# A tiled transpose: hand-made synchronisation, 256-byte aligned tiles, and stores that read 16 KB at a time

## The chip, the cores and the metric

The kernel runs on one core of a Trainium2 chip. The metric is the time of one execution on the device in microseconds (us), taken over several runs. A second number, the span, is the length of the profiled execution; in one and the same run the time is about 1.8 us longer than the span.

A ratio between two kernels is the mean time of one kernel's fast runs over the mean of the other's fast runs of the same rounds, so it is not quite the ratio of the medians that stand beside it.

## The reference

```python
def setup_inputs():
    return {"x": np.random.randn(8192, 8192).astype(np.float32)}

def reference(x):
    return np.transpose(x)
```

There are 268 MB to read and 268 MB to write, 537 MB through the DMA engines, and no arithmetic.

## The kernel before

The matrix is cut into 32 blocks of 1024 x 2048. A block is loaded by two DMAs whose contiguous runs are 8 KB (2048 floats of a row of `x`). TensorE transposes it in 128 x 128 pieces, eight to a PSUM tile of 128 x 1024. ScalarE (ACT) and VectorE (DVE) in turn copy these tiles to SBUF. Four copies fill an output tile, in which every partition holds four rows of 4 KB; one DMA stores it. A scheduler places the tiles and makes the semaphores.

```python
    R, C, G, LS = 8, 16, 4, 2          # (four lines in the kernel)
    I, J = R * P, C * P                # 1024 x 2048
    const_pool = ctx.enter_context(tc.tile_pool(name="const", bufs=1))
    in_pool = ctx.enter_context(tc.tile_pool(name="in_pool", bufs=2))
    out_pool = ctx.enter_context(tc.tile_pool(name="out_pool", bufs=4))
    psum_pool = ctx.enter_context(tc.tile_pool(name="psum", bufs=4, space=bass.MemoryType.PSUM))
    ident = const_pool.tile([P, P], dt)
    # ... cut: for each block
            in_tile = in_pool.tile([P, R, J], dt)
            for s in range(LS):
                src = x[i0 + s * rs * P:i0 + (s + 1) * rs * P, j0:j0 + J]
                src = src.rearrange("(a p) j -> p a j", p=P)
                nc.sync.dma_start(out=in_tile[:, s * rs:(s + 1) * rs, :], in_=src)
            for g in range(C // G):
                out_tile = out_pool.tile([P, G, I], dt)
                # ... cut: four times eight transposes into ps, one copy of ps to out_tile
                dst = out[j0 + g * G * P:j0 + (g + 1) * G * P, i0:i0 + I]
                dst = dst.rearrange("(b q) i -> q b i", q=P)
                nc.scalar.dma_start(out=dst, in_=out_tile)
```

Two facts about addresses matter. The first SBUF bytes of the kernel's own are four small constants (128 bytes) and the identity (512 bytes), so every input and output tile begins 128 bytes past a multiple of 256 (in the built program the first input tile lies at byte 17024 of a partition, 66 x 256 + 128). And although the four rows of an output tile lie side by side in SBUF, the stores are recorded as 65536 packets of 4096 bytes, one for each row.

## Time and profile before

| | before |
|---|---|
| time, median of the first 3 runs | 1279.18 us |
| span | 1276.3 us |
| DMA rate over the span | 421 GB/s |
| PE, DVE, ACT busy | 55%, 25%, 20% |

From the page of the kernel before: the mean busy share of the 16 DMA engines in tenths and the rate, each in 40 equal slices of the span; then the two queues with packets, MB and the time of their packets as a share of 16 engines (q1 is the loads, q10 the stores); then, for each kind of DMA, how many, the size and the median time from issue to landing.

```profile
DMA  9999999999999999999999999999999999999999
GB/s 392 425 423 424 425 423 425 423 422 424 423 422 423 424 424 423 424 422 423 424 424 422 422 422 424 424 423 423 423 423 424 422 422 422 424 424 423 422 422 375
...
q10 hardware_dynamic: 67584, 268.44, 51.4%
q1 hardware_dynamic: 33792, 268.44, 49.8%
...
in_tile<-in_x_dram SPq DMA_DIRECT2D x64, 4096.0 KB, 27.9
out_dram<-out_tile ACTq DMA_DIRECT2D x128, 2048.0 KB, 28.9
```

The engines that move data are busy 90% or more in every slice, and the rate is flat. This is a DMA-bound kernel: only a higher steady rate, or less time at the two ends, can shorten it.

The waits of the kernel before (who waited for what: us in total, times, longest):

```profile
ACT out_tile L69 <- DMA out_dram<-out_tile: 832.2, 97, 14.2
PEld ps L63 <- DVE out_tile L71: 605.9, 247, 9.7
DVE out_tile L71 <- DMA out_dram<-out_tile: 593.7, 81, 11.7
```

The copies wait for stores to give output tiles back. So stores lag and loads are ahead: a backlog of stores is queued. By the packet records stores move at least 119 GB/s in every 2 us from 32 to 1274 us.

The end of the kernel before, in five stretches of its span (stretch; length; busy time and number of instructions for PE, PEld, DVE, ACT, POOL; granted clock; DMA share; GB/s):

```profile
1210.00:1230.00 20.00, 9.03 (x40) 8.12 (x40) 3.67 (x3) 3.85 (x4) 0.00 (x0) 0.63 1.02 426
1230.00:1240.00 10.00, 6.78 (x39) 6.02 (x38) 3.67 (x3) 1.93 (x2) 0.00 (x0) 0.71 1.02 419
1240.00:1250.00 10.00, 7.33 (x62) 6.38 (x59) 3.99 (x4) 4.05 (x4) 0.00 (x0) 1.00 1.02 421
1250.00:1260.00 10.00, 6.77 (x56) 6.06 (x56) 4.58 (x4) 3.44 (x4) 0.00 (x0) 1.00 1.03 419
1260.00:1280.00 20.00, 1.09 (x8) 0.86 (x8) 1.23 (x2) 0.61 (x1) 0.00 (x0) 0.62 0.66 271
```

The packet records put the end of the last load's data at 1232.8 us. For 27 us after it, to 1260 us, the DMA engines still run at about 420 GB/s: the backlog covers the time in which the last block is transposed.

### The profile page before, as it was taken

Reading aid. Unit: us, or ns where it says so; the run is one execution under the profiler, and the core shown is the slowest. Engines: PE = TensorE matmul, PEld = TensorE weight load, DVE = VectorE, ACT = ScalarE, POOL = GpSimd, SP = SyncE. Lnnn points to the kernel's source line nnn. Section 1 sums busy time; section 2 is a strip of 40 time slices with the busy share of each in tenths; the row PEclk is TensorE's granted clock in tenths of the full one; section 3 lists DMA queues with packets and bytes.
Section 4 is the critical chain, followed back from the end, with each engine's and each line's share of the span. In section 5 each row is a group of like instructions: output and inputs, shape, how many; then the busy total and the mean of one; then the engine's idle time right before and its main releaser. Section 6 shows DMA issues by size and latency. Waiting matters only on the chain.

```text
span 1276.3 us, 9511 instructions
## 1 busy us (share of the span) xinstructions
PE 700.7 (55%) x4096; PEld 629.0 (49%) x4096; DVE 313.5 (25%) x256; ACT 252.8 (20%) x257; POOL 0.7 (0%) x6
## 2 busy tenths in 40 slices
PE   3555555655565545655556555555555655556463
PEld 3454455544554544544445554454444544445453
DVE  1222223222232222322123221222222322122222
ACT  1221112121121211212112121221211212112121
POOL 0000000000000000000000000000000000000000
PEclk8777777767777677776677766878667777677867
DMA  9999999999999999999999999999999999999999
GB/s 392 425 423 424 425 423 425 423 422 424 423 422 423 424 424 423 424 422 423 424 424 422 422 422 424 424 423 423 423 423 424 422 422 422 424 424 423 422 422 375
DMA packets 101418, 537.49 MB, mean 421 GB/s; under 512 B 3072, under 2 KB 3072, under 8 KB 68608
## 3 DMA queue, kind: packets, MB, share of 16 engines
q10 hardware_dynamic: 67584, 268.44, 51.4%
q1 hardware_dynamic: 33792, 268.44, 49.8%
q8 instruction: 32, 0.52, 0.1%
q14 instruction: 10, 0.08, 0.0%
HBM read 268.44 MB, written 268.44 MB: 421 GB/s over the span
## 4 chain that ended last, share of the span: by engine, by line
DMA 89%; PE 6%; DVE 3%; issue 0%; ACT 0%; DVEq 0%; ACTq 0%; SPq 0%
DMA out_dram<-out_tile 87%; PE ps L63 6%; DVE out_tile L71 3%; DMA in_tile<-in_x_dram 2%; ACT out_tile L69 0%; DVEq L71 0%; ACTq L69 0%; SPq L55 0%
## 5 line engine op out<-in xcount | busy, mean ns | idle before, releaser
L63 PE MATMUL ps<-ident,in_tile 128*128 128x128 f32 x4096 | 700.7, 344 | 560.5 <-DVE out_tile L71 535.3
L63 PEld LDWEIGHTS ps<-ident,in_tile 128*128 128x128 f32 x4096 | 629.0, 181 | 631.9 <-DVE out_tile L71 605.9
L71 DVE COPY out_tile<-ps 128x1024 f32<-128x1024 f32 x256 | 313.5, 1225 | 948.9 <-DMA out_dram<-out_tile 593.7
L69 ACT COPY out_tile<-ps 128x1024 f32<-128x1024 f32 x256 | 251.5, 1014 | 1007.1 <-DMA out_dram<-out_tile 832.2
L69 ACT ACT_TABLE_LOAD x1 | 1.3, 1283 | 0.7 <-PEq L91 0.7
masks.py:199 POOL TENSOR_SCALAR_AFFINE_SELECT ident<-ident 128x128 f32<-128x128 f32 x1 | 0.3, 292 | 0.1
masks.py:197 POOL MEMSET ident<- 128x128 f32 x1 | 0.2, 204 | 0.3 <-POOLq L91 0.3
L91 POOL MEMSET const-bfloat16-1.0<- 128x1 bf16 x1 | 0.1, 101 | 0.0
L91 POOL MEMSET const-uint8-127<- 128x1 uint8 x1 | 0.1, 101 | 0.0
L91 POOL MEMSET const-float32-0.0<- 128x1 f32 x1 | 0.1, 98 | 0.2 <-issue 0.2
L91 POOL MEMSET const-float32-1.0<- 128x1 f32 x1 | 0.1, 98 | 0.0
## 6 DMA issues: line engine op xcount, KB each, us to landing
in_tile<-in_x_dram SPq DMA_DIRECT2D x64, 4096.0 KB, 27.9
out_dram<-out_tile ACTq DMA_DIRECT2D x128, 2048.0 KB, 28.9
```

The lines of the kernel that those rows point to most:

```text
L63: nc.tensor.transpose(ps[:, a * P:(a + 1) * P], in_tile[:, a, b * P:(b + 1) * P], ident,)
L69: nc.scalar.copy(out=out_tile[:, bb, :], in_=ps)
L71: nc.vector.tensor_copy(out=out_tile[:, bb, :], in_=ps)
L91: nc = _bacc.Bacc("TRN2", target_bir_lowering=False, num_devices=1)
```

## The change

The intent is to raise the DMA rate. The tiles are allocated by hand behind a pad of 128 bytes, so that they are 256-byte aligned (the first input tile now lies at byte 17152, 67 x 256). A store is given a source of one 16 KB run for each partition and a destination of four 4 KB rows. The last store stays as it was. Semaphores are written by hand. Tile sizes, numbers of buffers, loads and arithmetic are the same. The core of the diff, with cuts marked:

```diff
+def wide_dma(nc, eng, queue, out, in_):
+    return eng.add_instruction(
+        mybir.InstDMACopy(mode="Copy", name=nc.get_next_instruction_name(), engine=eng.engine,
+            ins=[physical(in_)], outs=[physical(out)], queue=queue))   # physical(): cut
...
-    ident = const_pool.tile([P, P], dt)
-    make_identity(nc, ident)
+    with tc.tile_critical():
+        nc.alloc_sbuf_tensor("pad", [P, 32], dt)
+        ident = nc.alloc_sbuf_tensor("ident", [P, P], dt).ap()
+        ins = [nc.alloc_sbuf_tensor(f"in_tile{k}", [P, R, J], dt).ap() for k in range(NIN)]
+        outs = [nc.alloc_sbuf_tensor(f"out_tile{k}", [P, G * I], dt).ap() for k in range(NOUT)]
+        pss = [nc.alloc_psum_tensor(f"ps{k}", [P, I], dt).ap() for k in range(NPS)]
...
+            if k >= NIN:
+                nc.sync.wait_ge(s_pe, (k - NIN + 1) * C)
...
+                    if n >= NPS:
+                        nc.tensor.wait_ge(s_cp[(n - NPS) % 2], (n - NPS) // 2 + 1)
...
+                    if bb < 2 and ouse > 0:
+                        eng.wait_ge(s_st[ob], 16 * ouse)
...
-                nc.scalar.dma_start(out=dst, in_=out_tile)
+                if ng < NG:
+                    st = wide_dma(nc, nc.scalar, "qActDynamicHW", dst, outs[ob])
+                else:
+                    st = nc.scalar.dma_start(out=dst, in_=outs[ob])
+                st.then_inc(s_st[ob], 16)
```

More of the change, by code (lines that the diff above doesn't have):

```diff
@@ L8, with physical @@
 from concourse._compat import with_exitstack
+def physical(ap):
+    t = ap.tensor
+    dims = [list(d) for d in ap.ap]
+    if len(dims) == 2:
+        dims.insert(1, [dims[1][1], 1])
+    return mybir.PhysicalAccessPattern(
+        ap=dims,
+        offset=ap.offset,
+        dtype=ap.dtype,
+        memref=t.name,
+        memsetref=t.name + "_set",
+    )
+def wide_dma(nc, eng, queue, out, in_):
+    return eng.add_instruction(
+        mybir.InstDMACopy(
+            mode="Copy",
+            name=nc.get_next_instruction_name(),
+            engine=eng.engine,
+            ins=[physical(in_)],
+            outs=[physical(out)],
+            queue=queue,
+        )
+    )
 @with_exitstack
@@ L30 @@
     LS = 2
-    const_pool = ctx.enter_context(tc.tile_pool(name="const", bufs=1))
-    in_pool = ctx.enter_context(tc.tile_pool(name="in_pool", bufs=2))
-    out_pool = ctx.enter_context(tc.tile_pool(name="out_pool", bufs=4))
-    psum_pool = ctx.enter_context(tc.tile_pool(name="psum", bufs=4, space=bass.MemoryType.PSUM))
-    ident = const_pool.tile([P, P], dt)
-    make_identity(nc, ident)
-    n_bi = N // I
-    n_bj = M // J
-    copy_idx = 0
-    for bj in range(n_bj):
-        j0 = bj * J
-        for bi in range(n_bi):
-            i0 = bi * I
-            in_tile = in_pool.tile([P, R, J], dt)
-            rs = R // LS
+    NIN = 2
@@ new lines @@
+    NOUT = 4
+    NPS = 4
+    with tc.tile_critical():
[4 more added lines that the diff above has]
+        pss = [nc.alloc_psum_tensor(f"ps{k}", [P, I], dt).ap() for k in range(NPS)]
+        s_id = nc.alloc_semaphore("s_id")
+        s_ld = [[nc.alloc_semaphore(f"s_ld{k}_{s}") for s in range(LS)] for k in range(NIN)]
+        s_st = [nc.alloc_semaphore(f"s_st{k}") for k in range(NOUT)]
+        s_pe = nc.alloc_semaphore("s_pe")
+        s_cp = [nc.alloc_semaphore("s_cpa"), nc.alloc_semaphore("s_cpv")]
+        nc.gpsimd.memset(ident, 0.0).then_inc(s_id, 1)
+        nc.gpsimd.wait_ge(s_id, 1)
+        nc.gpsimd.affine_select(
+            out=ident,
+            in_=ident,
+            compare_op=mybir.AluOpType.not_equal,
+            fill=1.0,
+            base=0,
+            pattern=[[-1, P]],
+            channel_multiplier=1,
+        ).then_inc(s_id, 1)
+        nc.tensor.wait_ge(s_id, 2)
+        blocks = [(bi, bj) for bj in range(M // J) for bi in range(N // I)]
+        rs = R // LS
+        n = 0
+        ng = 0
+        NG = len(blocks) * (C // G)
+        for k, (bi, bj) in enumerate(blocks):
+            slot, use = k % NIN, k // NIN
+            i0, j0 = bi * I, bj * J
+            in_tile = ins[slot]
+            if k >= NIN:
+                nc.sync.wait_ge(s_pe, (k - NIN + 1) * C)
@@ L52 @@
             for s in range(LS):
                 src = x[i0 + s * rs * P:i0 + (s + 1) * rs * P, j0:j0 + J]
-                src = src.rearrange("(a p) j -> p a j", p=P)
-                nc.sync.dma_start(out=in_tile[:, s * rs:(s + 1) * rs, :], in_=src)
+                nc.sync.dma_start(
+                    out=in_tile[:, s * rs:(s + 1) * rs, :],
+                    in_=src.rearrange("(a p) j -> p a j", p=P),
+                ).then_inc(s_ld[slot][s], 16)
             for g in range(C // G):
-                out_tile = out_pool.tile([P, G, I], dt)
+                ob, ouse = ng % NOUT, ng // NOUT
@@ L59 @@
+                ng += 1
                 for bb in range(G):
                     b = g * G + bb
-                    ps = psum_pool.tile([P, R * P], dt)
+                    ps = pss[n % NPS]
+                    e = n % 2
+                    eng = (nc.scalar, nc.vector)[e]
+                    if n >= NPS:
+                        nc.tensor.wait_ge(s_cp[(n - NPS) % 2], (n - NPS) // 2 + 1)
                     for a in range(R):
-                        nc.tensor.transpose(
+                        if b == 0 and a % rs == 0:
+                            nc.tensor.wait_ge(s_ld[slot][a // rs], 16 * (use + 1))
+                        ins_t = nc.tensor.transpose(
@@ L67 @@
                         )
-                    if copy_idx % 2 == 0:
-                        nc.scalar.copy(out=out_tile[:, bb, :], in_=ps)
-                    else:
-                        nc.vector.tensor_copy(out=out_tile[:, bb, :], in_=ps)
-                    copy_idx += 1
+                    ins_t.then_inc(s_pe, 1)
+                    eng.wait_ge(s_pe, n + 1)
+                    if bb < 2 and ouse > 0:
+                        eng.wait_ge(s_st[ob], 16 * ouse)
+                    o = outs[ob][:, bb * I:(bb + 1) * I]
+                    if e == 0:
+                        c = nc.scalar.copy(out=o, in_=ps)
+                    else:
+                        c = nc.vector.tensor_copy(out=o, in_=ps)
+                    c.then_inc(s_cp[e], 1)
+                    n += 1
                 dst = out[j0 + g * G * P:j0 + (g + 1) * G * P, i0:i0 + I]
+                nc.scalar.wait_ge(s_cp[0], n // 2)
+                nc.scalar.wait_ge(s_cp[1], n // 2)
                 dst = dst.rearrange("(b q) i -> q b i", q=P)
-                nc.scalar.dma_start(out=dst, in_=out_tile)
+                if ng < NG:
[3 more added lines that the diff above has]
+                st.then_inc(s_st[ob], 16)
+        for ob in range(NOUT):
+            nc.sync.wait_ge(s_st[ob], 16 * (ng // NOUT))
 _INS = ['x']
```

## The prediction

> What bounds it now. The slice table of the profile page has the DMA engines at 90% or more in all 40 slices and 422 to 425 GB/s in all but the first (392) and last (375). PE is busy 55%, DVE 25%, ACT 20%; the chain of waits that ended last is 87% stores. So the 16 DMA engines are the limit. The queue table gives loads 49.8% of their time for 32768 packets of 8 KB (310 ns each) and stores 51.4% for 65536 of 4 KB (160 ns). In the trace's packet records 8 KB loads start 306 ns apart and 4 KB stores 155.3 ns apart on an engine, with a small bubble every few packets.
>
> [...] bubbles cost about 3 ns per load and 1 per store.
>
> What the change does. (1) Tiles now start 128 bytes off a 256-byte boundary (512-byte identity behind 128 bytes of constants); the pad aligns them. [...] the runtime's own 8 KB packets take 309 ns beside the loads, as these do. So I am unsure that alignment helps. (2) A store reads 16 KB once and writes four rows: [...] (3) Hand-made semaphores make PE, ACT and DVE wait for exactly what they need; they matter only after the last load lands. Loads, tiles, buffers and arithmetic stay.
>
> Costs, estimated from those packets, per engine 2048 loads and 4096 store rows: 2048 x 309 + 4096 x 156 = 1272 us now. [...]
>
> What is given back. With both queues full, loads now move 283 GB/s and stores 140: the engine alternates packets, 8 KB against 4 KB. If it alternates 16 KB against 8 KB, stores win two thirds, the backlog of stores that covers the tail is gone, and after the last load the DMA waits for the first four tiles: 4 x 0.86 us of PE and a 1.23 us copy, 5 us.
>
> Sum: both gains and the tail loss 1257 us, without the loss 1252; stores alone 1267 and 1262; no gain, up to 1284. I say 1260 us, 1.5% faster; 8 in 10 within 1247 to 1277. Chances: faster by over 2% 0.30, within 2% 0.66, slower 0.04.
>
> What would show it. Steady slices at 428 to 432 GB/s. Store packets below 153 ns per 4 KB, about 610 ns if recorded as 16 KB. Loads at 305 ns if alignment matters, unchanged if not. More waits of PE for loads, fewer of ACT and DVE for stores; a last slice below 375 GB/s if the tail loses.
>
> What would make it wrong. A cost per written row instead of per read: no gain from wide reads. [...] Alignment worth more than I see. A tail loss that does not come, or is larger because PE's clock is throttled.

Two terms of the sum are cut from this text, together with the ceiling that they were worked out from, because no run here shows the figures that they rest on: what the wide reads and what the aligned loads were each to save. By the totals that are left, they came to 17 us (1284 to 1267) and 10 us (1267 to 1257). With both, and with the 5 us given back at the end, the sum came to 1257 us; the forecast was 1260. The signs of 428 to 432 GB/s and of 153, 610 and 305 ns follow from the cut terms too.

## The result

| | before | changed |
|---|---|---|
| median time (4 runs each) | 1279.2 us | 1276.62 us |
| ratio, with 95% interval | | 0.9976 (0.996 to 0.9993) |
| span | 1276.3 us | 1275.1 us |
| DMA rate over the span | 421 GB/s | 421 GB/s |

The kernel became 0.24% faster where 1.5% was forecast. The lines of the changed kernel's page and waits that answer to those above:

```profile
DMA  9999999999999999999999999999999999999996
GB/s 393 417 430 426 426 427 428 428 430 426 429 425 428 429 427 430 426 426 430 427 427 429 427 429 425 428 421 426 429 427 428 425 426 429 428 427 428 427 398 269
...
q1 hardware_dynamic: 33792, 268.44, 49.9%
q10 hardware_dynamic: 18816, 268.44, 49.6%
...
in_tile<-in_x_dram SPq DMA_DIRECT2D x64, 4096.0 KB, 39.3
out_dram<-out_tile ACTq DMA_DIRECT2D x128, 2048.0 KB, 17.6
```

```profile
ACT out_tile L133 <- PE ps L122: 1007.6, 160, 29.6
DVE out_tile L135 <- PE ps L122: 947.2, 256, 30.4
PE ps L122 <- DMA in_tile<-in_x_dram: 734.1, 43, 26.2
```

Three things can be read here. The steady slices did rise, from about 423 to about 427 GB/s. The last two slices fell, from 422 and 375 to 398 and 269. And the roles have turned round: no compute engine waits for stores any more, PE waits 734 us for loads, a store lands after 17.6 us instead of 28.9 and a load after 39.3 instead of 27.9.

The same five stretches at the end of the changed kernel:

```profile
1210.00:1230.00 20.00, 12.39 (x114) 12.15 (x112) 9.30 (x8) 6.80 (x7) 0.00 (x0) 0.92 1.02 432
1230.00:1240.00 10.00, 0.00 (x0) 0.00 (x0) 0.00 (x0) 0.00 (x0) 0.00 (x0) 0.50 0.95 405
1240.00:1250.00 10.00, 5.99 (x40) 5.99 (x41) 2.26 (x2) 2.03 (x2) 0.00 (x0) 0.63 0.18 77
1250.00:1260.00 10.00, 9.40 (x87) 9.17 (x84) 6.87 (x7) 5.79 (x6) 0.00 (x0) 1.00 0.86 364
1260.00:1280.00 20.00, 0.00 (x0) 0.00 (x0) 0.67 (x1) 0.00 (x0) 0.00 (x0) 0.68 0.57 239
```

From 1230 to 1240 us no compute engine does anything, and from 1240 to 1250 us the DMA engines are 18% busy. Two lines of the timeline of that stretch (start, length, engine, line, operation) say why:

```profile
1244.01 15.39 PE L122 MATMUL ps<-ident,in_tile 128*128 128x128 f32 x124 [21.62 <-DMA in_tile<-in_x_dram]
...
1250.27 0.55 ACTq L29 DMA_DIRECT2D out_dram<-out_tile  x1
```

PE stood idle for 21.62 us until the last block had landed, and the first store of that block could be issued only 6.3 us later. By then all other stores were done: from 1248 to 1250 us the rate is 0 GB/s.

### How the packet records are read from here on

The page's averages are too coarse for the rest, so these quantities are worked out from the trace's packet records (start, length, size and queue of each packet), in the same way for every kernel:

- *steady*: bytes moved between 100 and 1200 us, each packet spread evenly over its recorded length, over the time. This way of counting gives about half a GB/s less than the page.
- *shares*: load rate and store rate in stretches of 2 us in which both exceed 100 GB/s, medians.
- *last load*: when the data of the last load packet ended, on the span's clock.
- *lost at the end*: for each 1 us from 1205 us to the last store packet, one minus the rate over the steady rate, summed.

| kernel | shares, load : store | steady GB/s | last load, us | lost at the end, us |
|---|---|---|---|---|
| before | 285 : 140 | 422.6 | 1232.8 | 3.2 |
| changed | 145 : 282 | 426.8 | 1242.9 | 12.7 |

These two rows account for the result. At the steady rates 536.9 MB take 1270.4 and 1257.9 us: 12.5 us gained. The end gives 9.5 us back. The same sum from 2 us, where the loads begin, to 40 us rises from 0.5 to 1.6 us, 1.1 more. That leaves 1.9 us; the spans differ by 1.2.

### The profile page after: what moved, and what is told of

The parts are those of the page before. It is cut to its first block, busy times and chain, and to the rows that moved or that the text cites. A ratio compares the mean times of both kernels' runs of the same rounds, so it can differ in the third digit from the quotient of the medians.

```text
span 1275.1 us, 9369 instructions
## 1 busy us (share of the span) xinstructions
PE 524.8 (41%) x4096; PEld 513.3 (40%) x4096; DVE 313.5 (25%) x256; ACT 251.3 (20%) x257; POOL 0.7 (0%) x6
## 4 chain that ended last, share of the span: by engine, by line
another core or an unknown queue 39%; DMA 32%; PE 28%; issue 0%; DVE 0%; ACT 0%; ACTq 0%; SPq 0%
DMA in_tile<-in_x_dram 32%; PE ps L122 28%; DVE out_tile L135 0%; ACT out_tile L133 0%; ACTq L29 0%; SPq L105 0%; SPq L174 0%; ACTq L130 0%; ACTq L140 0%; SPq L64 0%
## 5 line engine op out<-in xcount | busy, mean ns | idle before, releaser
L122 PE MATMUL ps<-ident,in_tile 128*128 128x128 f32 x4096 | 524.8, 296 | 734.6 <-DMA in_tile<-in_x_dram 734.1
L122 PEld LDWEIGHTS ps<-ident,in_tile 128*128 128x128 f32 x4096 | 513.3, 155 | 745.8 <-DMA in_tile<-in_x_dram 702.4
## 6 DMA issues: line engine op xcount, KB each, us to landing
in_tile<-in_x_dram SPq DMA_DIRECT2D x64, 4096.0 KB, 39.3
out_dram<-out_tile ACTq DMA_DIRECT2D x128, 2048.0 KB, 17.6
```

Of the source, the lines that this page charges most:

```text
L122: ins_t = nc.tensor.transpose(ps[:, a * P:(a + 1) * P], in_tile[:, a, b * P:(b + 1) * P], ident,)
```

## The experiments

The theory (A in the expectations): a DMA engine takes one packet of each queue in turn, so the larger packet gets the larger share (runs 7 and 9 test it). Wide stores overtake the loads, the backlog of stores vanishes, and the last block is exposed. The steady gain was to come from fewer read packets and from alignment. Rivals: the exact waits cause the loss at the end (B); alignment is worth nothing (C); the loss at the end has another cause (D); written rows cost something too (E). Every kernel below gave the correct result; the times are medians, the ratios are to the kernel before in the same rounds.

### 1 to 4: alignment, width and rewrite taken apart

Edits: `e1` is the changed kernel without pad and without wide stores; `e2` without wide stores; `e3` without pad; `e4` is the kernel before with a pad.

```diff
 e1, e3:
-        nc.alloc_sbuf_tensor("pad", [P, 32], dt)
 e1, e2:
-                if ng < NG:
+                if False:
 e4 (in the kernel before):
+    pad = const_pool.tile([P, 32], dt)
+    nc.gpsimd.memset(pad, 0.0)
     ident = const_pool.tile([P, P], dt)
```

> The hand-synchronised program alone: 4 KB reads, tiles 128 B off the boundary. Theory A (the tail loss comes from wide store packets winning two thirds of the engines): as before, 1279 us, steady 423 to 424 GB/s, last load's data in at about 1233 us, last but one slice above 415 GB/s. Rival B (the exact hand-made waits bring the tail loss): last load at 1240 us or later and a last slice below 300 GB/s, about 1288 us.

> Aligned tiles, 4 KB reads. Theory A: loads alone run at 428 GB/s as in the changed kernel (422 before), stores stay about 155 to 156 ns apart; steady 425 to 427 GB/s; loads win two thirds again, so no tail loss: 1268 to 1272 us, faster than the changed kernel. Rival C (alignment is worth nothing, the wide reads brought all of the steady gain): loads alone 422 GB/s, 1279 us. Rival B: tail loss stays, 1280 us or more.

> 16 KB reads, tiles 128 B off. Theory A: loads alone back at 422 GB/s, steady about 424 to 426, tail loss of some 11 us stays: 1280 to 1286 us. Rival C: steady 427.5, 1276 us as the changed kernel.

> The kernel before with 128 B of padding and nothing else. Theory A: as the hand-synchronised aligned narrow kernel within 2 us, 1268 to 1272 us: alignment alone gives the gain and the rewrite nothing. Rival C: 1279 us.

| kernel | time, us | ratio (95%) | loads alone, GB/s | shares | steady | last load | lost at the end |
|---|---|---|---|---|---|---|---|
| e1: rewrite alone | 1281.65 | 1.0021 (1.0009 to 1.0034) | 422.1 | 285 : 140 | 422.7 | 1236.2 | 5.2 |
| e2: rewrite, aligned | 1277.75 | 0.9995 (0.9982 to 1.0008) | 428.3 | 285 : 140 | 423.7 | 1230.5 | 5.3 |
| e3: rewrite, wide | 1275.0 | 0.9976 (0.9963 to 0.9988) | 422.0 | 146 : 281 | 426.4 | 1241.9 | 10.4 |
| e4: before, aligned | 1276.87 | 0.9988 (0.9974 to 1.0001) | 428.3 | 285 : 140 | 423.6 | 1230.7 | 4.4 |

"Loads alone" is the rate between 15 and 29 us, before any store has begun. The window view shows the same (12 to 28 us; it counts a packet where it starts) for the kernel before, `e4` and the changed kernel:

```profile
12.00:28.00 16.00, 8.79 (x43) 8.41 (x44) 2.45 (x2) 2.06 (x3) 0.00 (x0) 0.79 1.01 423
12.00:28.00 16.00, 8.73 (x51) 8.51 (x52) 2.54 (x3) 2.99 (x3) 0.00 (x0) 0.79 1.01 428
12.00:28.00 16.00, 6.39 (x40) 6.02 (x41) 1.89 (x2) 2.02 (x2) 0.00 (x0) 1.00 1.01 430
```

What follows. The rewrite gains nothing: `e1` is 0.2% slower than the kernel before, with 2 us more lost at the end. Rival B falls as the explanation of the large loss: with the same hand-made waits and 4 KB reads, loads keep two thirds, the last load is in by 1236 us, and 5 us are lost. Only `e3` and the changed kernel, which have wide reads, land the last load after 1240 us.

Alignment is real but hardly matters, and my expectation of 1268 to 1272 us for `e2` and `e4` was wrong, as was 1280 to 1286 us for `e3`. All three times lie within 2.2 us of those that rival C named (1279 and 1276 us), though its 422 GB/s for aligned loads alone did not come. Loads that have the engines to themselves go from 422.1 to 428.3 GB/s in both programs. But in these two programs they have them to themselves for the first 30 us only. In the stretches with both queues busy the mean sum rises from 423.4 (before) to 424.5 (`e4`), and the steady rate by 1.0. In time, `e4` cannot be told from the kernel before, nor `e3` from the changed kernel. Between `e1` and `e2`, which differ in the pad alone and ran in the same rounds, the gain does show: their intervals do not overlap, and the means are 3.4 us apart.

Stores gain nothing by the pad. In the narrow kernels they run alone for about 200 of the 1100 us between 100 and 1200 us, and then move 421.1 GB/s both in the kernel before and in `e4`, 420.7 in both `e1` and `e2`. So of the two directions only loads, which write the tiles, are faster for it; stores, which read the tiles, are not. Why the cost to loads nearly vanishes when both queues are busy is not shown by these runs.

Width gave the steady gain: from `e2` to the changed kernel it goes from 423.7 to 426.8 GB/s, 9.2 us of 1267. Not all of this is a lower cost of packets. In `e2` it was stores that ran alone, for 214 of the 1100 us, at 421 GB/s; in the changed kernel it is loads, for 190 us, at 428. With both queues busy the sum rises from 424.6 to 426.5 only. By these figures about half of the gain (an estimate) comes from which queue is left to run alone.

### 5 and 6: only the last stores narrow again

```diff
-                if ng < NG:
+                if ng <= NG - 8:      # e6: NG - 16
```

> The changed kernel with the last 8 of its 128 stores (two blocks) in 4 KB reads. Theory A (share goes by packet size): beside those stores loads move 285 GB/s instead of 144, the last load lands at about 1230 us instead of 1243, the loss at the end falls from 12.7 to about 5 us: 1268 to 1271 us. Rival D (the loss at the end has another cause[...]): the last load lands at 1240 us or later, 1275 us or more.

> As the last, with four blocks of 4 KB reads. Theory A: a backlog is rebuilt one block earlier, the last load lands at about 1220 to 1230 us, and the time is within 1.5 us of the last run: two blocks are enough. Rival D: 1275 us or more.

| kernel | time, us | ratio (95%) | steady | last load | lost at the end |
|---|---|---|---|---|---|
| e5: last 8 of 128 narrow | 1268.77 | 0.9923 (0.991 to 0.9937) | 426.7 | 1230.2 | 4.0 |
| e6: last 16 narrow | 1268.57 | 0.9923 (0.991 to 0.9937) | 426.8 | 1222.8 | 3.5 |

The end of `e5`, the same stretches:

```profile
1210.00:1230.00 20.00, 13.03 (x114) 12.79 (x112) 9.28 (x8) 6.80 (x7) 0.00 (x0) 0.93 1.01 423
1230.00:1240.00 10.00, 9.29 (x66) 9.29 (x67) 4.04 (x4) 3.95 (x4) 0.00 (x0) 0.75 1.02 420
1240.00:1250.00 10.00, 6.58 (x61) 6.34 (x59) 5.66 (x5) 3.85 (x4) 0.00 (x0) 0.94 1.02 419
1250.00:1260.00 10.00, 0.00 (x0) 0.00 (x0) 0.00 (x0) 0.00 (x0) 0.00 (x0) 0.50 1.02 420
1260.00:1280.00 20.00, 0.00 (x0) 0.00 (x0) 0.00 (x0) 0.00 (x0) 0.00 (x0) 0.76 0.13 54
```

Where the changed kernel moved 77 GB/s between 1240 and 1250 us, this one moves 419. Nothing but the width of the last eight stores differs (the very last was narrow already). PE has transposed the last block before 1250 us, and the stores queued behind it keep the engines busy until 1260. The theory's numbers came out, and rival D falls. The two runs agree within the noise: two blocks of narrow stores are enough.

### 7 and 9: stores that read 8 KB

If share goes by packet size, a store packet as large as a load packet must make it 1 to 1.

```diff
+                    half = outs[ob].rearrange("p (h f) -> p h f", h=2)
-                    st = wide_dma(nc, nc.scalar, "qActDynamicHW", dst, outs[ob])
+                    st = wide_dma(nc, nc.scalar, "qActDynamicHW", dst, half)
 e9 besides:
-                if ng < NG:
+                if ng <= NG - 8:
```

> Stores in 8 KB reads of two rows each, the size of a load packet. Theory A: with both queues full the two move the same, about 213 GB/s each; [...] steady two thirds of the way from 423.6 to 426.8 GB/s, 425.7; the loss at the end mostly gone, 5 to 7 us: 1269 to 1273 us. If share does not go by packet size: not 1 to 1, and the end as in the changed kernel.

> 8 KB reads, the last 8 stores in 4 KB reads: the two gains together. Theory A: steady 426.9 GB/s as with 8 KB reads, loss at the end about 4 us in place of 8.3: 1266 to 1268 us. If the rest of the loss at the end is not a matter of shares: 1271 us.

| kernel | time, us | ratio (95%) | shares | steady | last load | lost at the end |
|---|---|---|---|---|---|---|
| e7: 8 KB reads | 1271.32 | 0.9943 (0.9931 to 0.9956) | 217 : 210 | 426.9 | 1228.7 | 8.3 |
| e9: 8 KB reads, last 8 narrow | 1270.73 | 0.9934 (0.9922 to 0.9947) | 217 : 210 | 426.9 | 1226.5 | 7.1 |

The shares became 1 to 1, and the page of `e7` now has loads and stores landing after the same time:

```profile
in_tile<-in_x_dram SPq DMA_DIRECT2D x64, 4096.0 KB, 37.3
out_dram<-out_tile ACTq DMA_DIRECT2D x128, 2048.0 KB, 37.1
```

That the engines take turns packet by packet can be read from the records too. In stretches with both queues busy, the commonest time by far, apart from its multiples, from the start of any load packet to the start of a later one is 461 ns in the kernel before (as in `e2` and `e4`), 612 in `e7`, and 918 or 913 in the changed kernel; store packets give the same figures. Alone, an aligned load packet most often follows the last after 306 ns and a 4 KB store packet after 155. So 461 is one load and one store, 612 two packets of 8 KB, and 918 one of 8 KB and one of 16 KB.

The steady rate is that of the 16 KB reads, better than the 425.7 expected: reading 16 KB at a time in place of 8 brings nothing more (426.8 against 426.9 GB/s). The 8.3 us that `e7` lost at the end are more than the 5 to 7 expected. The end of `e9` missed its number: 7.1 us were lost where 4 were expected, and its time is the 1271 us named for the case that this rest is not a matter of shares. In 2 us bins from 1254 us its rate is 422, 418, 290, 256, 161 and 26 GB/s. The cause is not shown: the records do not name the engine of a packet, so they cannot tell whether some of the 16 engines ran out of work before others.

### 8 and 11: what a written row costs

Blocks of 512 x 4096 (`e8`) and of 2048 x 1024 (`e11`) keep the 16 KB reads but write eight rows of 2 KB or two of 8 KB. Load packets become 16 KB and 4 KB.

```diff
-    R = 8
-    C = 16
-    G = 4
+    R, C, G = 4, 32, 8        # e11: 16, 8, 2
 # cut: PSUM tiles stay 128 x 1024 and the loops over transposes follow
```

> Blocks of 512 x 4096 in place of 1024 x 2048: loads of 16 KB, stores of 16 KB reads into eight 2 KB rows. Theory A (a fixed cost per read packet, none per written row): loads 607 ns apart, stores as before at about 611 to 615 ns a packet, steady 428 to 430 GB/s, shares 1 to 1, little loss at the end: 1259 to 1267 us. Rival E (written rows cost too): store packets well above 615 ns, 630 or more, and steady below 424 GB/s, 1280 us or more.

> Blocks of 2048 x 1024: loads of 4 KB, stores of 16 KB reads into two 8 KB rows. A cost of about 2.25 ns per written row (615 ns with four rows, 624 with eight) gives store packets of 610 to 611 ns with two. Share by packet size gives loads one fifth, about 85 GB/s, beside stores, 340; the loss at the end is then at least that of the changed kernel, 12 us or more. If rows cost nothing, 615 ns.

`e8` took 1274.27 us (0.9971, 0.9958 to 0.9985) at a steady 424.9 GB/s with shares of 223 : 203. `e11` took 1280.7 us (1.0014, 1.0001 to 1.0028); in a stretch with both queues full (310 to 332 us) loads moved mostly 75 to 110 GB/s and stores 305 to 355 (over all stretches of 2 us in which both exceed 40 GB/s the medians are 95 and 333), the last load landed at 1249.9 us, and 12.8 us were lost at the end.

The most frequent recorded length of a 16 KB store packet, and the mean:

| rows written for each 16 KB read | kernel | most frequent, ns | mean, ns |
|---|---|---|---|
| 2 | e11 | 611 | 612.2 |
| 4 | changed | 615 | 615.8 |
| 8 | e8 | 624 | 625.5 |

Neither theory had this right for `e8`; 624 ns lies between "unchanged" and 630. From two rows to eight, a written row costs about 2 ns ((624 - 615) / 4 = 2.25). With that figure the 611 ns of `e11` was foretold before it ran. Between one row and two no cost is seen: an 8 KB store packet of `e7`, which writes two rows, is recorded at 309 ns like an 8 KB load packet, which writes one. And `e8` and `e11` also change the length of the rows and the size of the load packets, so that the number of rows is the cause is likely, not isolated. So eight short rows take away what larger loads bring: loads alone move 431.6 GB/s in `e8` and 428.3 in the changed kernel, but the steady rates are 424.9 and 426.8.

The loads that run alone give the cost of a packet by its size.

| load packets alone (15 to 29 us) | kernel | GB/s | ns a packet (16 x bytes / rate) | two packets of half the size less this one, ns |
|---|---|---|---|---|
| 4 KB, aligned | e11 | 421.8 | 155.4 | |
| 8 KB, aligned | changed | 428.3 | 306.0 | 4.8 |
| 16 KB, aligned | e8 | 431.6 | 607.4 | 4.6 |
| 8 KB, 128 B off | before | 422.1 | 310.5 | |

Two packets of 4 KB take 4.8 ns longer than one of 8 KB, and two of 8 KB 4.6 ns longer than one of 16 KB. So a load packet costs an estimated 4.6 to 4.8 ns beyond what grows with its bytes, and a bad alignment about as much again (310.5 less 306.0 is 4.5 ns).

### 10: the first stores narrow too

```diff
-                if ng < NG:
+                if 4 < ng <= NG - 8:
```

> 16 KB reads but for the first 4 and the last 8 stores. The changed kernel dips to 268 GB/s for about 2 us when its first wide store starts, and loses 1.6 us before 40 us, where the kernels with 4 KB reads lose 0.5. If the first wide descriptors cause it while the load queue is still starting, the dip goes or comes later while both queues are full: up to 1 us less than with only the last 8 narrow, 1267.5 to 1269 us.

It took 1268.06 us (0.9911, 0.9898 to 0.9925). The sum up to 40 us fell from 1.9 us (`e5`) to 0.9, as expected. But the interval overlaps that of `e5`, so a gain in time over `e5` is not shown. Both beat the kernel before, by 0.8 and 0.9%. The changed kernel ran in other rounds; set against its ratio of 0.9976, theirs are 0.5 and 0.7% lower.

## Why the prediction was wrong, point by point

- *DMA bounds the kernel; rewritten waits are off the critical path.* Right. `e1` moved the time by 0.2%, for the worse.
- *The same loss for both kinds of packet, by alignment or as a fixed cost.* There is a fixed cost for each load packet (an estimated 4.8 ns, 2 x 155.4 - 306.0, from aligned packets of 4 and 8 KB). The loss by misalignment (4.5 ns) comes on top of it, and I had counted it among the "bubbles" of 3 ns a load. It shows when loads run alone.
- *10 us by aligned loads.* Wrong in size: 1.0 GB/s of 422.6, an estimated 3 us; in time 3.4 us from `e1` to `e2`, and none clear of noise from the kernel before to `e4`. Loads were relieved of it while they ran alone (4.5 ns a packet), hardly beside stores (423.4 to 424.5 GB/s). The sign I named for it, the mean length of load packets in the queue table, could not show it: it stands at 310 ns in both kernels. A recorded length is not the distance from one packet to the next (306.0 ns for aligned loads alone).
- *17 us by wide reads.* The direction was right, the size was not: 9.2 us (`e2` against the changed kernel), of which about half is the change in what runs alone, a term that the sum did not have. Missing in the sum was also the written row: a store packet of 16 KB is recorded at 615 ns with four rows and at 611 with two (`e11`), over the 1024 such packets that 4096 rows make an estimated 4 us. The doubt was there ("a cost per written row instead of per read") but weighted as all or nothing.
- *"Stores win two thirds", the backlog that covers the tail is gone.* Right in mechanism and share: 145 : 282. The size was wrong: 5 us predicted, 9.5 us measured (12.7 against 3.2). The first four tiles took 6.3 us instead of 5, with PE's granted clock at 0.73 from 1244.0 to 1250.3 us. The rest lies before them: from 1238 to 1244 us, while the last load was still landing, the rate already fell from 349 to 141 GB/s in 2 us bins. Why is not shown, as the records do not name the engine of a packet. My sum had the full rate up to the end of that load.

The sum, then: minus 9 for width, minus 3 for alignment, plus 9.5 at the end and 1 at the start, about minus 2 us, against the forecast's minus 19 (1279 to 1260). The time stayed within the range, at its slow edge, because the range was wide and not because the sum was right: the forecast gain was six times the measured one. The step that failed is the balance of steady gain against tail loss: each gain was taken too large (17 and 10 us for 9 and 3) and the loss too small (5 us for 10.5, of which the start, 1, was not foreseen), and what is left of the gains nearly cancels against the loss.

## What to carry to other kernels

Where two DMA queues competed in these runs, the size of their packets set who got the bandwidth (8 against 4 KB 285 : 140 GB/s, 8 against 8 KB 217 : 210, 8 against 16 KB 145 : 282). So a change meant to make one transfer cheaper also made it win, and the loser decided how the kernel ended (the last load at 1242.9 us in place of 1232.8). Before you count a higher steady rate as time, ask which transfers will be left over after the last load has landed; here, making the last 8 of 128 stores narrow again turned 0.24% into 0.77%. And test a suspected packet cost in the state in which the kernel spends its time: alignment was worth 1.5% to loads alone (422.1 to 428.3 GB/s), nothing to stores alone (421.1 both times), and about a quarter of a per cent to the steady rate (422.6 to 423.6).
